# An encoder on one core: operand placement, the way into the MLP, PSUM banks, the head and the last down part rearranged

## The chip, the cores and the metric

The kernel runs on one core of a Trainium2 chip. The metric is device time in microseconds (us) of one launch. Engines are named as in the profile: PE is TensorE's matmul stream and PEld its weight loads, DVE is VectorE, ACT is ScalarE, POOL is GpSimd, SP is SyncE, whose queue issues most DMAs. A "q" behind a name (SPq) is that engine's own sequencer.

## The reference

Two encoder layers over 256 tokens of width 2048, with 256 memory tokens, all in float32. Cut to what matters:

```python
m = rms_norm(mem, mem_norm)
h = x
for i in range(2):
    n = rms_norm(h, attn_norm[i])
    # layer 0: 12 heads of 2-D neighbourhood attention with a bias; layer 1: grouped-query
    # attention with normalised, rotated q and k; both: 4 heads over the memory tokens (km, vm)
    z = n @ (a_w_in if i == 0 else b_w_in)
    km, vm = split(m @ w_mem_kv[i])
    h = h + concatenate([mix, cross]) @ w_o[i]
    n = rms_norm(h, mlp_norm[i])
    h = h + square(relu(n @ w_up[i])) @ w_down[i]      # 2048 -> 8192 -> 2048
return rms_norm(h, final_norm)
```

## The kernel before

**Numbers in two parts.** Every float32 matrix product is made of three products of rounded parts: each operand is split into a high part (`hi`, rounded on ACT by a copy, line 299) and a low part (`lo`, the rest, a subtraction on DVE, line 300), and hi·hi, hi·lo and lo·hi are summed in PSUM. Weights come from HBM in chunks of 128 x 2048 (1 MB, "raw") and are split in halves of 1024 columns. The normed inputs are split the same way and lie transposed, high and low side by side: `memT` (the memory), `nT` (input of a layer), `cat` (attention outputs), `hT` (input of the MLP). So each weight costs ACT and DVE one pass and PE three.

**Two kinds of product.** In "S" work (`s_products`, lines 211 to 222) the weights are stationary and the activations move: 512 wide against hi (line 218), 256 wide against lo (221). In "M" work (`m_products`, 198 to 209) the activations are stationary and the weights move, 512 wide: lines 205, 208, 209. The up projection (`u_products`, 664 to 672) has weights `uh`/`ul` stationary and `hT` moving, 256 wide: lines 670 to 672. In these names "moving operand" is the one that streams through PE, and the profile's matmul rows read `out<-moving,stationary`.

**The plan.** `run_all` (line 245) takes a list of pieces of work. Each has a load, a `pre` and a `prep` stage that are issued some pieces ahead (`ahead`, `SOON`), and a `run` stage with its matmuls. `later(n, ...)` puts small work n pieces ("ticks") behind. A scheduler orders what is written within the dependences; engines execute their own instructions in order.

**The stages.** The head (`begin`, 224) normalises `mem` and runs the first two chunks of the memory keys (`km`) side by side while their pieces of 256 KB arrive; then come the rest of the memory keys and values of both layers. Layer 0 makes qkv from `nT` and attends head by head; the output projection runs over `cat` (`add_o`, 644), 512 columns at a time; `o_done` (597) adds each result to h, and makes `hT` from the scaled h: copy by a scale on ACT (610), transposes on PE (317), split by gain on ACT and DVE (324, 325). The scale comes from the first three quarters of the columns, and `inv` (615) later corrects the output.

**The MLP.** Of 8 parts of d_ff, part 0's up products come first; then each step of parts 1 to 7's up products is interleaved with a down step of the part before (`add_mlp`, 887). A down step (`down_grains`, 740) is a 2 x 2 block product made in seven products (p1 to p7, Winograd's form): it loads four blocks of weights (b, t), makes sums of them (lines 758, 767, 768 on DVE, 759 by an accumulating DMA on POOL's queue), splits them into bh/bl and th/tl, and multiplies them with a_s, sums of the activation blocks, likewise split (`squared`, 716). The seven results stay in PSUM banks over half a part, and then go to h or to z (`taken`, 804; lines 802, 813, 815; `folded`, 820). The last part, part 7, is multiplied down in the plain way (`plain_grains`, 833): per 512 columns two chunks, the first split as two halves into the uh/ul buffers, the second as one piece of 2048 into th/tl, with a_p stationary. After that h is complete (`down_done`, 907), and in layer 1 `finish` (931) normalises and writes the last columns.

**Where things lie.** PSUM has 8 banks of 512 floats. `open_sums` (95) opens the pool `att` (4 banks, attention and transposes) and then `acc` (4 banks, sums). For parts 1 to 7 both are closed and one pool of 8 (`up` and p1 to p7) is opened (line 699). `wide` (418) holds nT0, hT0, nT1, hT1 one after the other; `half_of_side` (674) makes the uh/ul tiles, two buffers each.

Of the kernel before, what the change touches and what calls it, by code (L numbers as in the profile page):

```python
# [17 lines left out]
P = 128  # L18
# [16 lines left out]
HALF = CH // 2  # L35
GROUP = 2
PARTS = 8
PK = DFF // PARTS // P
STEPS = PK // 2
GUARD = 3  # L40
MASKED = -1e30

# [28 lines left out]
def encoder_kernel(ctx: ExitStack, tc: tile.TileContext, t: dict, out: bass.AP):  # L71
# [42 lines left out]
    mem0 = h.rearrange("p a b -> p (a b)")  # L114
    raws = [at.ring.tile([P, CH], F32, tag="raw", bufs=3, name=f"raw{c}") for c in range(2)]
    for j in range(8):
        s = slice(j * 512, (j + 1) * 512)
        nc.sync.dma_start(mem0[:, s], t["memT"][:, s])
        if j % 2 == 0:
            s = slice(j * 256, (j + 2) * 256)  # L120
            for c in range(2):
                nc.sync.dma_start(raws[c][:, s], t["w_km0"][c][:, s])
# [18 lines left out]
    def halves_of(w):  # L141

        tiles = {}

        def load():
            tiles["raw"] = loaded(w.src, "U")

        def prep_early(hf):
            tiles[hf] = half_of_side(tiles["raw"], hf)

        def prep(hf):
            if hf == 0:
# [24 lines left out]
        return [Grain(lambda: run(0), None, None, None, lambda: prep(0)),  # L177
                Grain(lambda: run(1), after, None, None, lambda: prep(1))]
# [45 lines left out]
    def begin():  # L224

        box["memT"] = at.cat.tile([P, KT, 512], F32R, tag="cat", name="memT")
        tiles = {}
        for w in plan[:2]:
            w.start(w)
        for q in range(4):  # L230
            for k in range(4 * q, 4 * q + 4):
                split_pair(box["memT"], mem0[:, k * SEQ : (k + 1) * SEQ], G_MEM, k)
                if k % 4 == 0:
                    for c, w in enumerate(plan[:2]):
# [4 lines left out]
            for c, w in enumerate(plan[:2]):  # L239
                s = slice(q % 2 * 512, q % 2 * 512 + 512)  # L240
                s_products(w, 4 * q, 4, *(x[:, s] for x in tiles[c]))
        for w in plan[:2]:
            w.done(w)

    def run_all():
        begin()
        for w in plan[2:]:
            order.extend([w] if isinstance(w, Grain) else halves_of(w))
# [25 lines left out]

    def add_m(srcs, acts, done):
        add_ms([(srcs, done)], acts, [(0, c) for c in range(len(srcs))])

# [3 lines left out]

    def add_ms(blocks, acts, order):

        ps = {}
        for n, (b, c) in enumerate(order):
            begins = all(o[0] != b for o in order[:n])

            def start(w, b=b, begins=begins):
                if begins:
                    ps[b] = [at.acc.tile([P, 512], F32, tag="acc", name="ps_m") for _ in range(NT)]  # L290
                w.ps = ps[b]
# [5 lines left out]
    def split(dst_hi, dst_lo, src):  # L297

        nc.scalar.activation(dst_hi, src, AF.Copy)  # L299
        nc.vector.tensor_tensor(dst_lo, src, dst_hi.bitcast(F32), op=ALU.subtract)  # L300

# [9 lines left out]
    def transposed(dst, src, ks, which):  # L311

        for a in range(0, len(ks), 2):
# [4 lines left out]
            for b, k in enumerate(ks[a : a + 2]):  # L318
                split_pair(dst, pt[:, b, :], which, k)

    def split_pair(dst, src, which, k):

        g = gain(which, k)
        nc.scalar.activation(dst[:, k, :SEQ], src, AF.Copy, scale=g)
        nc.vector.scalar_tensor_tensor(dst[:, k, SEQ:], src, g, dst[:, k, :SEQ].bitcast(F32),  # L325
                                       op0=ALU.mult, op1=ALU.subtract)
# [90 lines left out]

    def wide(name):
        return keep.tile([P, KT, 512], F32R, tag="wide", name=name)

# [60 lines left out]
    def add_mem(layer):  # L481
        for hd in range(NMH):
            add_s(t[f"w_km{layer}"][hd], get("memT"), km_done(layer, hd))
        add_m([t[f"w_vm{layer}"][c] for c in range(4)], parts_of("memT"), vm_done(layer))

# [98 lines left out]
    def sum_squares(which, i, nb):  # L584
        sq = at.side.tile([P, 512], BF16, tag="junk", bufs=2, name="sq")
        nc.scalar.activation(sq, h[:, i, nb * 512 : (nb + 1) * 512], AF.Square,
                             accum_out=ssq[which][:, i, nb : nb + 1])

    def mean_square(which, n, name):
# [5 lines left out]
        return v  # L595

    def o_done(layer, nb):
        which = 2 * layer

        def guard():  # L600
# [23 lines left out]
        def f(w):  # L624
            if nb == 0:
                closed("work")
                at.side = opened("side", side="right")
            for i in range(NT):
                hs = h[:, i, nb * 512 : (nb + 1) * 512]
                nc.vector.tensor_tensor(hs, w.ps[i], hs, op=ALU.add)  # L630
                if nb < 3:
                    sum_squares(which, i, nb)
            if nb == GUARD - 1:
                later(1, guard)
                for b in range(GUARD):
                    later(2 + 2 * b, scaled, b)
            if nb == 3:
# [46 lines left out]
    def up_grains(layer, part, m):  # L684
# [8 lines left out]
        def run(hf):  # L693
            if hf == 0:
                if part == 0:
                    own["ps"] = at.acc.tile([P, 512], F32, tag="acc", name="ps_u")[:, :SEQ]
                else:
                    if part == 1 and m == 0:
                        closed("ps_acc", "ps_att")
                        at.sums = opened("ps_sums", space=bass.MemoryType.PSUM)  # L700
# [39 lines left out]
    def down_grains(layer, part, n, begins, ends):  # L740
# [4 lines left out]
        def load():  # L745
# [4 lines left out]
            nc.sync.dma_start(own["t"][:, 0, :], src[:, 3 * 512 :])  # L750

        def block(k):

# [34 lines left out]
        def after_second():  # L788
# [44 lines left out]
    def plain_grains(layer, nb):  # L833
# [24 lines left out]
        def run(n):  # L858
# [5 lines left out]
            for i in range(NT):  # L864
                m_products(w, k0, nk, i, *own[c, hf], n == 0, n == 2)

        def after():
# [5 lines left out]
            for i in range(NT):  # L873
                for n, (c, hf, k0, nk) in enumerate(PIECES):
                    m_products(w, k0, nk, i, *own[c, hf], n == 0, n == 2, keep_order=True)
                w.done(w, i)

        return [Grain(lambda: run(0), None, lambda: load(0), None, lambda: prep(0, 0), SOON),
                Grain(lambda: run(1), None, None, None, lambda: prep(0, 1), SOON),
                Grain(lambda: run(2), after, lambda: load(1), None, lambda: prep(1, 0), SOON)]  # L880

# [25 lines left out]
    def down_done(layer, nb):  # L907
        def f(w):
# [161 lines left out]
    for j in range(8):  # L1070
        later(1 + j // 2, mem_squares, j)
    later(2, lambda: pin(nc.sync.dma_start(ident, t["ident"])))
    later(5, mem_stats)
    later(21, x_load)
# [124 lines left out]
```

## Time and profile before

| | |
|---|---|
| median of 3 runs | 2072.03 us (2071.43 to 2072.48) |
| the profiled execution | 2069.22 us, span 2067.2 us |
| granted TensorE clock in it | 0.997 |
| PE busy | 2039.7 us, 99% of the span |
| DVE busy | 1668.6 us, 81% |
| ACT busy | 1251.3 us, 61% |
| bytes moved | 433.78 MB, mean 210 GB/s |

How to read it: times are microseconds from the span's start. A row of the timeline gives start, duration, engine, line, operation, `out<-in`, and how many it groups; in brackets stands the idle time before it and what ended it. A duration of a matmul is longer than the time from its start to the next one's start, since they are pipelined; the pace is read from starts. A waits row gives the instruction that waited, what it waited for, the sum, the number and the longest of the waits. In the windows table a stretch is followed by its length, busy time and number of instructions of each engine, the granted clock of PE (1.00 is full), the share of DMA time, and GB/s.

### The profile page before, as it was taken

To read this page: it belongs to the slowest core of one execution; us is meant where nothing else is said; L and a number is where in the kernel's file an instruction comes from. 1 tells how busy PE (TensorE), PEld (TensorE's weight loads), DVE (VectorE), ACT (ScalarE), POOL (GpSimd) and SP (SyncE) were. 2 spreads that over 40 slices of the span, in tenths; PEclk is the share of its full clock that TensorE was granted. 3 is DMA by queue.
4 is the path that set the end of the run, shared out by engine and by line. 5 is a ranking of instruction groups with operands and counts; after the bars stand their busy time and mean duration, and the time that the engine had idled before them with its cause. 6 is when DMAs were issued, how large, how long until landed. Compare 5 with 4: busy or idle time off the path is not lost.

```text
span 2067.2 us, 31544 instructions
## 1 busy us (share of the span) xinstructions
PE 2039.7 (99%) x12516; PEld 1815.0 (88%) x12516; DVE 1668.6 (81%) x2047; ACT 1251.3 (61%) x1642; POOL 119.2 (6%) x144
## 2 busy tenths in 40 slices
PE   8999999999999999999999999999999999999998
PEld 6888888889999999999988888889999999999996
DVE  6767667566899999999996667666988999999896
ACT  6755555555666666666656557555666666666653
POOL 0000000000010000010000001000000000000000
PEclk9999999999999999999999999999999999999999
DMA  7755555736777787787765454536877787777773
GB/s 266 297 183 177 189 175 170 274 105 202 223 235 231 218 240 225 225 240 226 231 201 209 171 177 143 188 138 197 232 227 227 224 242 222 233 232 223 232 225 121
DMA packets 92996, 433.78 MB, mean 210 GB/s; under 512 B 10416, under 2 KB 12080, under 8 KB 59568
## 3 DMA queue, kind: packets, MB, share of 16 engines
q1 hardware_dynamic: 75456, 399.25, 57.3%
q0 software_dynamic: 16816, 31.46, 8.6%
q8 instruction: 98, 1.61, 0.3%
q10 hardware_dynamic: 576, 1.05, 0.1%
q14 instruction: 50, 0.41, 0.1%
HBM read 398.17 MB, written 4.19 MB: 195 GB/s over the span
## 4 chain that ended last, share of the span: by engine, by line
PE 97%; DVE 1%; issue 1%; DMA 1%; ACT 0%; SPq 0%; POOLq 0%; POOL 0%; DVEq 0%; ACTq 0%
PE ps_u L672 11%; PE ps_u L670 11%; PE ps_u L671 11%; PE p L779 9%; PE p L780 9%; PE p L781 9%; PE ps_m L205 8%; PE ps_m L208 8%; PE ps_m L209 8%; PE ps_s L218 7%; PE ps_s L221 3%; PE pt_a L379 1%; PE pt_n L317 0%; PE av L387 0%; PE sc_ps L353 0%
## 5 line engine op out<-in xcount | busy, mean ns | idle before, releaser
L671 PE MATMUL ps_u<-hT,uh 128*128 128x256 f32 x2048 | 569.3, 278 | 3.7 <-DVE hT L325 3.6
L670 PE MATMUL ps_u<-hT,uh 128*128 128x256 f32 x2048 | 569.9, 278 | 1.5 <-ACT uh L299 1.5
L672 PE MATMUL ps_u<-hT,ul 128*128 128x256 f32 x2048 | 569.3, 278 | 1.5 <-DVE ul L300 1.3
L299 ACT ACTIVATE uh<-raw_U 128x1024 fp32r<-128x1024 f32 x278 | 295.0, 1062 | 325.2 <-PE ps_u L671 301.9
L300 DVE TENSOR_TENSOR lo<-raw,hi 128x1024 fp32r<-128x1024 f32 (+1 forms) x222 | 266.3, 1204 | 167.7 <-ACT hi L299 166.4
L671 PEld LDWEIGHTS ps_u<-hT,uh 128*128 128x128 f32 x2048 | 385.9, 188 | 9.1 <-DVE hT L325 4.5
L670 PEld LDWEIGHTS ps_u<-hT,uh 128*128 128x128 f32 x2048 | 386.3, 189 | 7.6 <-ACT uh L299 1.9
L672 PEld LDWEIGHTS ps_u<-hT,ul 128*128 128x128 f32 x2048 | 387.1, 189 | 3.0 <-DVE ul L300 2.3
L300 DVE TENSOR_TENSOR ul<-raw_U,uh 128x1024 fp32r<-128x1024 f32 x278 | 337.9, 1219 | 35.4 <-ACT uh L299 35.4
L299 ACT ACTIVATE hi<-raw 128x1024 fp32r<-128x1024 f32 (+1 forms) x222 | 231.3, 1047 | 218.7 <-PE ps_m L209 116.1
L299 ACT ACTIVATE th<-t 128x2048 fp32r<-128x2048 f32 x112 | 215.2, 1921 | 124.9 <-PE p L781 118.2
L300 DVE TENSOR_TENSOR tl<-t,th 128x2048 fp32r<-128x2048 f32 x112 | 256.3, 2288 | 40.3 <-ACT th L299 39.9
L300 DVE TENSOR_TENSOR bl<-b,bh 128x1536 fp32r<-128x1536 f32 x112 | 196.1, 1751 | 0.4
L780 PE MATMUL p<-tl,a_s 128*128 128x512 f32 x448 | 177.2, 396 | 0.0
L781 PE MATMUL p<-th,a_s 128*128 128x512 f32 x448 | 174.4, 389 | 0.0
L299 ACT ACTIVATE bh<-b 128x1536 fp32r<-128x1536 f32 x112 | 166.2, 1484 | 6.4
L779 PE MATMUL p<-th,a_s 128*128 128x512 f32 x448 | 166.1, 395 | 0.0
L759 POOL DMA_DIRECT2D t<-b x112 | 97.0, 866 | 1168.3 <-DVE t L758 377.5
L218 PE MATMUL ps_s<-nT,hi 128*128 128x512 f32 x448 | 141.7, 394 | 0.0
L781 PE MATMUL p<-bh,a_s 128*128 128x512 f32 x336 | 131.1, 390 | 0.0
L780 PE MATMUL p<-bl,a_s 128*128 128x512 f32 x336 | 130.9, 390 | 0.0
L758 DVE TENSOR_TENSOR t<-t,b 128x512 f32<-128x512 f32 x112 | 77.2, 690 | 48.2 <-DMA t<-in_w_pair 36.4
(235 smaller groups left out, 3510.6 us busy)
## 6 DMA issues: line engine op xcount, KB each, us to landing
raw_U<-in_w_up SPq DMA_DIRECT2D x128, 1024.0 KB, 6.6
b<-in_w_pair SPq DMA_DIRECT2D x112, 768.0 KB, 4.5
raw<-in_w_o SPq DMA_DIRECT2D x32, 1024.0 KB, 5.0
t<-in_w_pair SPq DMA_DIRECT2D x112, 256.0 KB, 3.4
t<-b POOLq DMA_DIRECT2D x112, 256.0 KB, 6.6
raw<-in_w_b SPq DMA_DIRECT2D x21, 1024.0 KB, 5.0
raw<-in_w_av SPq DMA_DIRECT2D x12, 1024.0 KB, 4.9
raw<-in_w_aq SPq DMA_DIRECT2D x12, 1024.0 KB, 4.9
```

What stands on the lines that cost most here:

```text
L205: first = nc.tensor.matmul(w.ps[i], ah, hi[:, s], start=st, stop=False)
L208: nc.tensor.matmul(w.ps[i], ah, lo[:, s], start=False, stop=False)
L209: nc.tensor.matmul(w.ps[i], al, hi[:, s], start=False, stop=sp)
L218: nc.tensor.matmul(ps, hi[:, s], acts[:, k0 + j, :], start=k0 + j == 0, stop=False)
L299: nc.scalar.activation(dst_hi, src, AF.Copy)
L300: nc.vector.tensor_tensor(dst_lo, src, dst_hi.bitcast(F32), op=ALU.subtract)
L670: nc.tensor.matmul(ps, hi[:, s], acts[:, k, :SEQ], start=k == 0, stop=False)
L671: nc.tensor.matmul(ps, hi[:, s], acts[:, k, SEQ:], start=False, stop=False)
L672: nc.tensor.matmul(ps, lo[:, s], acts[:, k, :SEQ], start=False, stop=k == KT - 1)
L779: nc.tensor.matmul(ps, a[:, 0, ai, :], hi[:, s], start=begins, stop=False)
L780: nc.tensor.matmul(ps, a[:, 0, ai, :], lo[:, s], start=False, stop=False)
L781: nc.tensor.matmul(ps, a[:, 1, ai, :], hi[:, s], start=False, stop=ends)
```

## The change

1. **Moving operands elsewhere.** `wide` takes a byte offset: nT0 and nT1 begin 480 bytes into a tile that has grown by 512; hT0 and hT1 stay at its start. `half_of_side` takes one too: uh/ul tiles grow by 256 bytes, and where they are moving operands (the first w_b chunks and the plain part) they begin `MOVING_AT` = 160 bytes in. One of two "junk" buffers goes.
2. **Head.** `begin` runs three chunks side by side instead of two; the third buffer of "raw" is used from the start. The work behind it gets other ticks, and the sums of layer 0's memory values come from the att banks.
3. **PSUM.** `acc` is opened ahead of `att`, so it has banks 0 to 3 instead of 4 to 7.
4. **Way into the MLP.** The old h of the last 512 columns is scaled ahead (`begun`); when the last output product is there, one operation per tile adds it, scaled, to that straight from PSUM, and the transposes follow. The add to h itself, its squares and `inv` come 4, 6 and 8 ticks later and are issued behind the last hT split (`past`). The first two down steps' sums and splits are issued behind a split of up weights (`behind`).
5. **Plain part.** The second chunk is split in two halves too, into own tiles with the tags bh/bl and th/tl, and the work is four pieces instead of three.

```diff
-    def wide(name):
-        return keep.tile([P, KT, 512], F32R, tag="wide", name=name)
+    def wide(name, at=0):
+        room = keep.tile([P, KT * 512 + P], F32R, tag="wide", name=name)
+        return room[:, at // 4 : at // 4 + KT * 512].rearrange("p (a b) -> p a b", b=512)
...
-    def half_of_side(raw, hf):
-        tiles = tuple(at.side.tile([P, HALF], F32R, tag=n, bufs=2, name=n) for n in ("uh", "ul"))
-        split(*tiles, raw[:, hf * HALF : (hf + 1) * HALF])
+    def half_of_side(raw, hf, place=0):
+        s = slice(place // 4, place // 4 + HALF)
+        tiles = tuple(at.side.tile([P, HALF + 64], F32R, tag=n, bufs=2, name=n)[:, s] for n in ("uh", "ul"))
+        box.setdefault("splits", []).append(split(*tiles, raw[:, hf * HALF : (hf + 1) * HALF]))
         return tiles
...
-            tiles[hf] = half_of_side(tiles["raw"], hf)
+            tiles[hf] = half_of_side(tiles["raw"], hf, MOVING_AT)
...
-            box["nT"] = wide("nT0")
+            box["nT"] = wide("nT0", 480)
...
-                box["nT"] = wide("nT1")
+                box["nT"] = wide("nT1", 480)
...
     def open_sums():
+        at.acc = opened("ps_acc", space=bass.MemoryType.PSUM, bufs=4)
         at.att = opened("ps_att", space=bass.MemoryType.PSUM, bufs=4)
-        at.acc = opened("ps_acc", space=bass.MemoryType.PSUM, bufs=4)
...
+FIRST_CHUNKS = 3
...
-        for w in plan[:2]:
+        for w in plan[:FIRST_CHUNKS]:
...
-                later((5, 5, 1, 1)[hd], put, w)
+                later((12, 12, 13, 8)[hd], put, w)
...
+    def past(fn, ins=None):
+
+        a, v = ins or box["ready"]
+        with tc.issue_after(a.ins), tc.issue_after(v.ins):
+            fn()
...
+        def begun():
+
+            y = at.side.tile([P, NT, 512], F32, tag="T", bufs=2, name="h_s")
+            for i in range(NT):
+                nc.scalar.activation(y[:, i, :], h[:, i, D - 512 :], AF.Copy, scale=box["scale"][:, i : i + 1])
+            box["begun"] = y
...
             if nb == 3:
-                later(1, scaled, 3)
+                y = box["begun"]
                 for i in range(NT):
-                    sum_squares(which, i, nb)
-                later(2, inv)
+                    nc.vector.scalar_tensor_tensor(y[:, i, :], w.ps[i], box["scale"][:, i : i + 1], y[:, i, :],
+                                                   op0=ALU.mult, op1=ALU.add)
+                box["ready"] = transposed(box["hT"], lambda i, k: y[:, i, k % 4 * P : (k % 4 + 1) * P],
+                                          list(range(12, KT)), (G_M0, G_M1)[layer])
+                later(4, past, add)
+                later(6, past, squares)
+                later(8, past, inv)
...
+        def behind(fn):
+
+            return (lambda: past(fn, box["splits"][-4])) if part == 0 and n < 2 else fn
...
-        return [Grain(lambda: run("first", FIRST), lambda: after(FIRST), load, pre, prep_first, SOON),
-                Grain(lambda: run("second", SECOND), after_second, None, None, prep_second, SOON)]
+        return [Grain(lambda: run("first", FIRST), lambda: after(FIRST), load, behind(pre), behind(prep_first), SOON),
+                Grain(lambda: run("second", SECOND), after_second, None, None, behind(prep_second), SOON)]
...
-                own[c, hf] = half_of_side(own[0], hf)
+                own[c, hf] = half_of_side(own[0], hf, MOVING_AT)
             else:
-                own[c, hf] = tuple(at.mlp.tile([P, CH], F32R, tag=x, name=x) for x in ("th", "tl"))
-                split(*own[c, hf], own[1])
-
-        PIECES = ((0, 0, 0, 2), (0, 1, 2, 2), (1, 0, 4, 4))
+                own[c, hf] = tuple(at.mlp.tile([P, HALF], F32R, tag="bt"[hf] + x, name=f"{x}_p") for x in "hl")
+                split(*own[c, hf], own[1][:, hf * HALF : (hf + 1) * HALF])
+
+        PIECES = ((0, 0, 0, 2), (0, 1, 2, 2), (1, 0, 4, 2), (1, 1, 6, 2))
```

More of the change, by code (lines that the diff above doesn't have):

```diff
@@ L114, in encoder_kernel @@
     mem0 = h.rearrange("p a b -> p (a b)")
-    raws = [at.ring.tile([P, CH], F32, tag="raw", bufs=3, name=f"raw{c}") for c in range(2)]
+    raws = [at.ring.tile([P, CH], F32, tag="raw", bufs=3, name=f"raw{c}") for c in range(FIRST_CHUNKS)]
     for j in range(8):
@@ L120, in encoder_kernel @@
             s = slice(j * 256, (j + 2) * 256)
-            for c in range(2):
+            for c in range(FIRST_CHUNKS):
                 nc.sync.dma_start(raws[c][:, s], t["w_km0"][c][:, s])
@@ L233, in begin @@
                 if k % 4 == 0:
-                    for c, w in enumerate(plan[:2]):
+                    for c, w in enumerate(plan[:FIRST_CHUNKS]):
                         if q % 2 == 0:
@@ L246, in run_all @@
         begin()
-        for w in plan[2:]:
+        for w in plan[FIRST_CHUNKS:]:
             order.extend([w] if isinstance(w, Grain) else halves_of(w))
@@ L273, in add_s, with add_m, add_ms @@
         plan.append(Work("S", src, acts, 0, True, True, start, done))
-    def add_m(srcs, acts, done):
-        add_ms([(srcs, done)], acts, [(0, c) for c in range(len(srcs))])
+    def add_m(srcs, acts, done, banks=None):
+        add_ms([(srcs, done)], acts, [(0, c) for c in range(len(srcs))], banks)
     def parts_of(name):
         return lambda k, i: tuple(box[name][:, k, b * SEQ + i * P : b * SEQ + (i + 1) * P] for b in range(2))
-    def add_ms(blocks, acts, order):
+    def add_ms(blocks, acts, order, banks=None):
         ps = {}
@@ L289, in start @@
                 if begins:
-                    ps[b] = [at.acc.tile([P, 512], F32, tag="acc", name="ps_m") for _ in range(NT)]
+                    pool, tag = (at.att, "att") if banks else (at.acc, "acc")
+                    ps[b] = [pool.tile([P, 512], F32, tag=tag, name="ps_m") for _ in range(NT)]
                 w.ps = ps[b]
@@ L318, in transposed @@
             for b, k in enumerate(ks[a : a + 2]):
-                split_pair(dst, pt[:, b, :], which, k)
+                last = split_pair(dst, pt[:, b, :], which, k)
+        return last
     def split_pair(dst, src, which, k):
         g = gain(which, k)
-        nc.scalar.activation(dst[:, k, :SEQ], src, AF.Copy, scale=g)
-        nc.vector.scalar_tensor_tensor(dst[:, k, SEQ:], src, g, dst[:, k, :SEQ].bitcast(F32),
+        first = nc.scalar.activation(dst[:, k, :SEQ], src, AF.Copy, scale=g)
+        return first, nc.vector.scalar_tensor_tensor(dst[:, k, SEQ:], src, g, dst[:, k, :SEQ].bitcast(F32),
                                        op0=ALU.mult, op1=ALU.subtract)
@@ L483, in add_mem @@
             add_s(t[f"w_km{layer}"][hd], get("memT"), km_done(layer, hd))
-        add_m([t[f"w_vm{layer}"][c] for c in range(4)], parts_of("memT"), vm_done(layer))
+        add_m([t[f"w_vm{layer}"][c] for c in range(4)], parts_of("memT"), vm_done(layer), layer == 0)
     mem_sq = at.work.tile([P, 512], F32, tag="b_o", bufs=3, name="mem_sq")
@@ L627, in f, with add, squares @@
                 at.side = opened("side", side="right")
[L628 to L631, printed above, removed]
+            def add():
+                for i in range(NT):
+                    hs = h[:, i, nb * 512 : (nb + 1) * 512]
+                    nc.vector.tensor_tensor(hs, w.ps[i], hs, op=ALU.add)
+            def squares():
+                for i in range(NT):
                     sum_squares(which, i, nb)
+            if nb < 3:
+                add()
+                squares()
             if nb == GUARD - 1:
@@ L864, in run @@
             for i in range(NT):
-                m_products(w, k0, nk, i, *own[c, hf], n == 0, n == 2)
+                m_products(w, k0, nk, i, *own[c, hf], n == 0, n == 3)
         def after():
@@ L879, in plain_grains @@
                 Grain(lambda: run(1), None, None, None, lambda: prep(0, 1), SOON),
-                Grain(lambda: run(2), after, lambda: load(1), None, lambda: prep(1, 0), SOON)]
+                Grain(lambda: run(2), None, lambda: load(1), None, lambda: prep(1, 0), SOON),
+                Grain(lambda: run(3), after, None, None, lambda: prep(1, 1), SOON)]
     SOON = (8, 5, 4)
```

20 lines of the change are left out of this document (11 added, 9 removed).

## The prediction

> **What bounds the kernel now.** I read the page's chain first, then the windows by stage, then TensorE's waits.
>
> ```profile
> PE 97%; DVE 1%; issue 1%; DMA 1%; ACT 0%; SPq 0%; POOLq 0%; POOL 0%; DVEq 0%; ACTq 0%
> ...
> L671 PE MATMUL ps_u<-hT,uh 128*128 128x256 f32 x2048 | 569.3, 278 | 3.7 <-DVE hT L325 3.6
> ```
> ```profile
> 26.00:449.00 423.00, 423.00 (x2265) 363.31 (x2264) 282.67 (x422) 233.52 (x388) 3.15 (x4) 1.00 0.56 199
> 449.00:460.00 11.00, 7.94 (x53) 6.72 (x53) 9.07 (x16) 6.52 (x10) 0.88 (x1) 0.95 0.65 169
> 460.00:1073.00 613.00, 613.00 (x4168) 563.88 (x4168) 551.09 (x594) 390.39 (x401) 47.01 (x54) 1.00 0.76 226
> ...
> 1387.00:1398.50 11.50, 7.87 (x54) 6.67 (x54) 9.25 (x17) 6.54 (x10) 0.90 (x1) 0.96 0.68 161
> ```
> TensorE (PE) carries 97% of the chain. In the windows (length, then busy time of PE, PEld, DVE, ACT and POOL) it is busy without a gap over long stretches: 423.00 of 423.00, 613.00 of 613.00. It loses time in two ways only: at a few places it waits, and where it is busy its matmuls start one after the other at a pace that isn't everywhere the same. The waits:
>
> ```profile
> PE ps_s L218 <- ACT hi L299: 8.5, 2, 7.0
> PE ps_u L671 <- DVE hT L325: 3.6, 2, 2.1
> PE ps_u L670 <- ACT uh L299: 1.5, 2, 0.8
> PE ps_m L208 <- DVE tl L300: 1.3, 1, 1.3
> PE ps_u L672 <- DVE ul L300: 1.3, 2, 0.6
> ```
> Apart from the first 7.0 us, which no part of the change shortens, these waits (in us, with their number and the longest) come to 9.2 us. The pace is in this table, whose windows run from the start of one matmul to the start of the last of an unbroken run (length, PE busy, instructions touched; those that began before and still ran are taken off: two after 256-wide ones, else one):
>
> ```profile
> 57.26:79.43 22.17, 22.17 (x128) 1.00 0.89 368
> 202.87:213.36 10.49, 10.49 (x47) 1.00 0.49 148
> 338.55:347.84 9.29, 9.29 (x55) 1.00 0.40 121
> 387.26:428.96 41.70, 41.70 (x186) 1.00 0.70 274
> 714.28:719.58 5.30, 5.30 (x46) 1.00 0.94 283
> 1941.96:1947.31 5.35, 5.35 (x48) 1.00 0.95 279
> 2012.52:2017.89 5.37, 5.37 (x24) 1.00 0.91 340
> 2018.14:2023.38 5.24, 5.24 (x24) 1.00 0.59 205
> ```
> At the same granted clock (1.00), 512-wide matmuls cost 10.49/45 = 233.1 ns with nT stationary (203 us), 41.70/184 = 226.6 with cat stationary (387 us), 5.37/23 = 233.5 for uh/ul over a_p (2012 us) and 5.24/23 = 227.8 for th/tl over the same a_p (2018 us). Shapes and weight loads are equal; what differs is where the two operands lie. In the built program hi/lo, cat, memT, th/tl and a_p begin at byte 128 modulo 512 of a partition, nT at 160 and uh/ul at 480. So the pairs at 227 have equal remainders and those at 233 don't. The 256-wide products over hT have two paces too, 5.35/47 = 113.8 (1942 us) and 5.30/45 = 117.8 (714 us), with the same addresses: there the pace is not decided by addresses alone.
>
> **The change, part by part, against the profiled execution (2069.22 us; its span is 2067.2).** PE's chain is the sum, so I add what each part takes from or gives to PE.
>
> *A. nT moved by 480 bytes* (to remainder 128). M products over nT: 12 w_av and 21 w_b chunks of 24 matmuls, 792, each 233.1 − 226.6 = 6.5 ns: −5.1 us. Bounds: nothing (if the pace isn't set by this) and −5.1. S products, of both widths, start every 9.29/53 = 175.3 ns over nT (339 us) and 22.17/127 = 174.6 over memT (57 us): 28 chunks of 32, 896 × 0.7 ns, −0.6.
>
> *B. uh/ul as moving operands at +160 bytes.* 8 plain half-loads with 24 matmuls and three early w_b chunks, 264 × (233.5 − 227.8 = 5.7 ns) = −1.5. The tiles grow by 256 bytes, so the second buffer of each lies 256 off the first: only half may reach remainder 128. Bounds −1.5 and 0; I take −1.3, nearer the full row.
>
> *C. Way into the MLP.* Starts of the matmuls in layer 0:
>
> ```profile
> 453.58 0.28 PE L670 MATMUL ps_u<-hT,uh 128*128 128x256 f32 x1
> 454.61 0.39 PE L670 MATMUL ps_u<-hT,uh 128*128 128x256 f32 x1 [0.75 <-ACT uh L299]
> 454.83 0.28 PE L671 MATMUL ps_u<-hT,uh 128*128 128x256 f32 x1
> 456.64 0.38 PE L671 MATMUL ps_u<-hT,uh 128*128 128x256 f32 x1 [1.54 <-DVE hT L325]
> ...
> 457.86 0.28 PE L672 MATMUL ps_u<-hT,ul 128*128 128x256 f32 x1
> 458.77 0.55 PE L672 MATMUL ps_u<-hT,ul 128*128 128x256 f32 x1 [0.63 <-DVE ul L300]
> ```
> ```profile
> 453.23 0.69 DVE L758 TENSOR_TENSOR t<-t,b 128x512 f32<-128x512 f32 x1 [1.62 <-DMA t<-in_w_pair]
> 453.84 2.29 DVE L300 TENSOR_TENSOR tl<-t,th 128x2048 fp32r<-128x2048 f32 x1
> ```
> Against 0.12 per start, the three gaps lose 0.9, 1.7 and 0.8 us; with smaller ones around 450 us about 4.3. DVE, in order, sits behind a DMA of pair weights (1.62) and its 2.29 us split before it may make hT. The window of layer 1 at 1387 (11.50 us, 7.87 busy) is of the same kind, so about 9 us for two layers. The change puts the first two pair steps behind that hT split (`past`), scales the old h beforehand and adds straight from PSUM. What is late next: the split of up weights, 1.06 on ACT and then 1.22 on DVE, which waits for a buffer that PE frees. I leave 1.7 us per layer for it: −5.9 (bounds 0 and −9). The h add, squares and inv that are put off have DVE and ACT time in the stage after (551 of 613 us busy on DVE, 390 on ACT); if that cover goes, the 3 us or so of them (two adds like the 0.69 row, two squares, inv) delay the first down products.
>
> *D. Head, three chunks side by side.*
>
> ```profile
> 22.02 0.73 PE L218 MATMUL ps_s<-memT,hi 128*128 128x512 f32 x2 [1.42 <-ACT hi L299]
> 23.28 0.50 PE L221 MATMUL ps_s<-memT,lo 128*128 128x256 f32 x2 [0.53 <-DVE lo L300]
> ```
> After two chunks PE waits for the third's split, 1.42 and 0.53 us, and some 0.3 more in the matmuls that restart (0.50 us against 0.40 and less). With three, PE has half as much again to do in each quarter, and 5 loads of 256 KB instead of 4 to wait for, so the first 7.03 us stay and the same gap comes one chunk later: ACT still clears the sums of PSUM and splits chunk 3 (1.05, then 1.2 on DVE), while chunk 3's load, now behind raw0's last split on SP's queue, has come. About 1.4: −0.9 (bounds −2.3, and +1.5 if that load is late).
>
> *E. PSUM order.* The waits for h L802 and z L813, at the plain part of layer 0 only, come of ps_m lying in banks that p4 and p5 still hold. Their two starts come 0.62 and 1.11 us after the one before instead of 0.23 and lose 1.3:
>
> ```profile
> 1073.42 0.39 PE L781 MATMUL p<-th,a_s 128*128 128x512 f32 x1
> 1074.04 0.48 PE L205 MATMUL ps_m<-uh,a_p 128*128 128x512 f32 x1 [0.24 <-DVE z L813]
> ...
> 1075.29 0.40 PE L209 MATMUL ps_m<-uh,a_p 128*128 128x512 f32 x1
> 1076.40 0.50 PE L205 MATMUL ps_m<-uh,a_p 128*128 128x512 f32 x1 [0.72 <-DVE h L802]
> ```
> Other banks: −1.3. **It also adds a wait.** Between parts 0 and 1, p3 now takes the bank of the last up sums of part 0, two matmuls after them, and ACT splits uh before it empties that bank:
>
> ```profile
> 495.72 1.06 ACT L299 ACTIVATE uh<-raw_U 128x1024 fp32r<-128x1024 f32 x1 [1.62 <-PE ps_u L671]
> 496.68 0.36 ACT L723 ACTIVATE c<-ps_u 128x256 f32<-128x256 f32 x1
> ```
> From the freed buffer (495.7) to the end of the relu (497.0) are 1.3 us, less two matmuls: +1.2 in each layer, +2.4 (bounds 0 and +3). Behind p3's first stand 18 more p matmuls and then the rest of the up block; nothing on PE overtakes it.
>
> *F. Plain part in halves.* The last block waits 1.3 us for tl (list of waits), because th and tl are one 2048-wide split each. Halves in their own tags are free earlier and take half as long: −1.5, counting the start's delay (bounds 0 and −1.7).
>
> Sum: −5.1 − 0.6 − 1.3 − 5.9 − 0.9 − 1.3 + 2.4 − 1.5 = −14.2, so 2055.0 for a profiled execution. The median of the runs shown, 2072.03, lies 2.8 above the profiled one; so **2057.8**. My own range for this case is 2050 to 2066: A and B at nothing add 7, C at its ends +6 or −3.
>
> **The rivals.**
> 1. *The placement does nothing.* The pace could come of something else that differs between these stretches: in the 256-wide products it differs at equal addresses. Then A and B go and 2057.8 + 7.0 = 2064.8. Against it: th/tl and uh/ul over one a_p, back to back, in one layer. The Trainium skill, "TensorE: Matmul & The Clock Gate", section "Wait — 56ns, not 53.3ns?", gives the warm start-to-start time as the width over 2.4 GHz plus about 2.5 ns, 215.8 for 512, whatever the addresses; "SBUF — State Buffer", section "A bandwidth-pool intuition that's wrong (but worth ruling out)", gives the weight load a second, independent read port. By that rule this rival holds; the rows (226.6 and 233.1) agree with neither its figure nor its one pace.
> 2. *Half the up products slow down.* The 256 bytes of padding also move the second uh/ul buffer against hT in the 6144 up products (3 × 2048). If every block on it falls to the pace of the 714 us row: 3072 × 4.0 ns = +12.3, giving 2070.1, about no change. Against it: the blocks of before at 117.8 share their addresses with those at 113.8.
> 3. *All the up products slow down, and the kernel is slower.* Place: the up blocks of parts 1 to 7 as well. If the pace is decided by how a block enters, and the padding or the moved splits tip all of them: 6144 × 4.0 = +24.6, giving 2082.4. It decides from 14.2/24.6 = 58% of them on. For it: the pace of 117.8 occurs with no change of code. Against it: most blocks hold 113.8, and the order of the built program starts as many of them with ul as before (14 of 112 steps).
>
> **How the numbers follow.** A measurement of this kernel tells 0.2%, 4 us, from no change. Forecast 0.72, rival 1 0.13, rival 2 0.08, rival 3 0.07. The predicted time is the forecast's. The range 2049 to 2067 takes in the forecast's bounds and rival 1, and leaves rivals 2 and 3 and some ends of the forecast out. Faster: 0.70 of the forecast and 0.11 of rival 1, 0.81. Same: 0.02, 0.02 and 0.07 of rival 2, 0.11. Slower: 0.07 of rival 3 and 0.01 of rival 2, 0.08.
>
> **What would show it.** A: hi/lo over nT start every 226 to 228 ns. B: uh/ul over a_p too, perhaps on one buffer in two. C: no wait for hT by PE, one for uh or ul of about a microsecond. D: the wait for hi after three chunks, not two, and shorter. E: no wait for z or h at the plain part, a new one of p for the relu at each change from part 0 to 1. F: no wait for tl. The steady windows with 613.00 of 613.00 stay as long as before; if they grow by 6 or 12 us, rivals 2 or 3 hold and I am wrong.

## The result, and the profile after

| | before | changed |
|---|---|---|
| median of 4 runs | 2071.73 us (2070.39 to 2072.48) | 2054.27 us (2053.93 to 2054.78) |
| ratio | | 0.9917, 95% interval 0.9899 to 0.9934 |
| span of the profiled execution | 2067.2 us | 2052.1 us |

The changed kernel is 17.5 us faster by the medians and 15.1 by the two spans; 2057.8 was forecast, with 14.2 us off the profiled execution. The forecast held, and in the right order of size for most of its terms. Three things behind it did not: equal remainders are no general rule for the pace, one term was put to the wrong part alone, and a loss of clock behind the way into the MLP went unseen. Each experiment below came with executions of its own of the kernel before, whose medians are 2069.83 to 2071.17 us, so kernels of different experiments are compared by ratios or by stages. One execution of experiment 2's kernel took 2253.24 us at a granted clock of 0.848 and is left out of its numbers.

PE still carries the chain. Its waits in the changed kernel (what waited, for what, us in total, times, longest):

```profile
PE ps_s L221 <- ACT hi L303: 7.7, 2, 6.8
PE p L816 <- ACT c L756: 2.1, 2, 1.1
PE ps_u L704 <- DVE ul L304: 1.8, 3, 0.8
PE av L392 <- ACT pT L303: 1.0, 1, 1.0
PE ps_s L224 <- DVE lo L304: 0.5, 1, 0.5
```

The waits for hT, uh, tl, h and z are gone; ul is waited for in three places, 1.8 us in all; and p waits for c, the relu (line 756 now), once in each layer: the wait that was added. Lines have moved by 3 to 38, so 670 to 672 are 702 to 704 here, and 299 and 300 are 303 and 304.

The paces in the changed kernel, windows read as before (length, PE busy, instructions touched, granted clock, DMA share, GB/s):

```profile
201.12:211.33 10.21, 10.21 (x47) 1.00 0.52 144
452.92:485.57 32.65, 32.64 (x287) 1.00 0.61 202
1140.37:1149.43 9.06, 9.06 (x41) 1.00 0.33 108
...
1959.99:1965.35 5.36, 5.36 (x48) 1.00 0.83 232
1999.64:2042.93 43.29, 43.29 (x192) 1.00 0.35 128
```

Over nT: 10.21/45 = 226.9 ns in layer 0 and 9.06/40 = 226.5 in layer 1, where the stretch of before had 233.1. The whole plain part of layer 1, uh/ul pieces and the others, is one run of 192 matmuls without a break, 43.29/191 = 226.6 ns, over both uh/ul buffers. The steady up products stay at 5.36/47 = 114.0.

The way into the MLP, which lost 0.9, 1.7 and 0.8 us at 453 to 459 us, in the changed kernel:

```profile
451.67 0.39 PE L702 MATMUL ps_u<-hT,uh 128*128 128x256 f32 x1
451.89 0.28 PE L703 MATMUL ps_u<-hT,uh 128*128 128x256 f32 x1
452.93 0.38 PE L704 MATMUL ps_u<-hT,ul 128*128 128x256 f32 x1 [0.76 <-DVE ul L304]
```

This is the one large gap that is left there: 1.04 us from start to start, 0.9 lost to the up weights' split. With the small ones of 0.2 to 0.4 us before and after it, the starts between 442 and 454 us are 1.76 us late in all; counted in the same way, those of before were 5.29 late between 444.5 and 459.5 us. And there the loss of before did not end. These are its windows right behind the last large gap of each layer, and then those behind the way in of the changed kernel:

```profile
459.50:462.20 2.70, 2.70 (x15) 0.50 0.93 291
1398.50:1401.00 2.50, 2.50 (x14) 0.52 0.91 282
```
```profile
454.00:470.00 16.00, 16.00 (x144) 1.00 0.58 197
1386.00:1400.00 14.00, 14.00 (x121) 1.00 0.55 201
```

In the kernel before the granted clock was 0.50 and 0.52 there, and the up products started about 0.21 us apart (459.55, 459.76, 459.97) instead of 0.113: about 1.2 us more in each layer. In the changed kernel it stayed at 1.00. Counted against 113.4 ns for each of the first 100 up products, the starts are 6.6 and 7.0 us late in the two layers of before, and 1.9 and 2.0 in the changed kernel.

The head, where the wait now stands behind three chunks:

```profile
24.86 0.40 PE L224 MATMUL ps_s<-memT,lo 128*128 128x256 f32 x2
26.13 0.73 PE L221 MATMUL ps_s<-memT,hi 128*128 128x512 f32 x2 [0.87 <-ACT hi L303]
```

And the wait that was added, in layer 0:

```profile
488.85 0.28 PE L702 MATMUL ps_u<-hT,uh 128*128 128x256 f32 x1
488.97 0.28 PE L703 MATMUL ps_u<-hT,uh 128*128 128x256 f32 x1
490.31 0.50 PE L816 MATMUL p<-bh,a_s 128*128 128x512 f32 x1 [1.06 <-ACT c L756]
```
```profile
488.93 1.06 ACT L303 ACTIVATE uh<-raw_U 128x1024 fp32r<-128x1024 f32 x1 [0.23 <-PE ps_u L703]
489.90 0.37 ACT L756 ACTIVATE c<-ps_u 128x256 f32<-128x256 f32 x1
```

From 488.97 to 490.31 are 1.34 us instead of 0.12: 1.2 lost, because ACT does 1.06 us of uh first.

**Where the time came from.** The next table cuts PE's time at the same instructions in each trace (the first S product over nT0, the first M over cat, the first up product of a layer, the first plain product of a layer, the last matmul's end). Over the kernels of all experiments, the attention, projection and last plain stages repeat within 0.1 us where nothing in them differs, so the table tells parts apart there that medians of runs cannot. Two stages repeat less well: the memory products take 92.95 to 94.23 us with the same three chunks, and an up-and-pair stage of the same code 626.00 to 626.93, for a reason that is left open below; 0.8 us of layer 1's 626.92 is of this kind.

| stage, us | before | changed | difference | parts in it |
|---|---|---|---|---|
| to the first matmul | 7.03 | 6.78 | −0.25 | |
| memory products | 94.28 | 93.06 | −1.22 | head |
| layer 0, attention | 249.07 | 247.85 | −1.23 | nT0 |
| output projection of layer 0 | 94.42 | 94.40 | −0.02 | |
| layer 0, up and pair steps | 629.24 | 626.09 | −3.15 | way in, PSUM |
| layer 0, plain part, and layer 1, attention | 199.62 | 194.95 | −4.67 | nT1, uh/ul, PSUM |
| output projection of layer 1 | 109.62 | 109.59 | −0.03 | |
| layer 1, up and pair steps | 629.24 | 626.92 | −2.31 | way in, PSUM |
| layer 1, plain part | 46.18 | 43.68 | −2.50 | uh/ul, halves |

### The profile page after: what moved, and what is told of

Read it like the earlier page. It is cut to its first block, busy times and chain, and to the rows that moved or that the text cites. A ratio compares the mean times of both kernels' runs of the same rounds, so it can differ in the third digit from the quotient of the medians.

```text
span 2052.1 us, 31583 instructions
## 1 busy us (share of the span) xinstructions
PE 2029.9 (99%) x12516; PEld 1812.2 (88%) x12516; DVE 1669.2 (81%) x2061; ACT 1252.7 (61%) x1652; POOL 119.3 (6%) x144
## 4 chain that ended last, share of the span: by engine, by line
PE 97%; ACT 1%; DVE 1%; issue 0%; DMA 0%; SPq 0%; POOLq 0%; POOL 0%; ACTq 0%
PE ps_u L704 11%; PE ps_u L702 11%; PE ps_u L703 11%; PE p L816 9%; PE p L817 9%; PE p L818 9%; PE ps_m L208 8%; PE ps_m L211 8%; PE ps_m L212 8%; PE ps_s L221 6%; PE ps_s L224 3%; PE pt_a L384 1%; PE pt_n L321 1%; DMA raw<-in_w_km 0%; PE av L392 0%
## 5 line engine op out<-in xcount | busy, mean ns | idle before, releaser
L303 ACT ACTIVATE hi<-raw 128x1024 fp32r<-128x1024 f32 (+1 forms) x224 | 231.7, 1039 | 210.4 <-PE ps_m L212 117.8
```

Of the source, the lines that this page charges most:

```text
L303: first = nc.scalar.activation(dst_hi, src, AF.Copy)
```

## The experiments

My theory was the prediction's: each part acts on its own stage, the pace is set by equal remainders, and the stalls at the way in come of the order on DVE and ACT. The rivals stand in each expectation.

**1. nT back (e1_nT_back).** The changed kernel with
```diff
-            box["nT"] = wide("nT0", 480)
+            box["nT"] = wide("nT0")
```
and the same for nT1.

> The changed kernel with nT0 and nT1 back at the start of their tiles (remainder 160 against 128 of hi and lo); all else as changed. Theory (the pace is set by where the two operands lie): M matmuls over nT go from about 227 to 233 ns, 792 of them, so 4.2 us of pace come back and the time is 2058.5 +- 0.7. Rival (the pace comes of something else in these stretches, the shift was idle): 2054.3, and the matmuls over nT stay at 227.

Measured: 2058.96 us, ratio to before 0.9946 (0.9932 to 0.9961). Its windows of the same two stretches:

```profile
201.37:211.86 10.49, 10.49 (x47) 1.00 0.48 147
1142.16:1151.49 9.33, 9.33 (x41) 1.00 0.31 109
```

10.49/45 = 233.1 and 9.33/40 = 233.3 ns, as before. The stage of layer 0's attention is 249.08 instead of 247.85, that with layer 1's attention 198.06 instead of 194.95: 1.2 + 3.1 = 4.3 us for the two offsets. The placement does it; the rival (the shift was idle) falls.

**2. Placement alone (e2_place_only).** The kernel before with `wide(name, at)`, 480 for nT0 and nT1, the padded uh/ul tiles with 160 where they move, and one junk buffer.

> The kernel before with the placement alone: nT0 and nT1 480 bytes in, uh and ul tiles 256 bytes larger and 160 bytes in where they move, one junk buffer. Theory: 4.2 us over nT and 1.6 us over a_p and for the first w_b chunks, so 5.8 us faster than before, 2066. Rival (the buffer 256 bytes off keeps 233): 5.0 us. Rival (no effect of placement): as before, 2071.7. The waits for hT, z, h and tl stay as in the kernel before in every case.

Measured: 2063.98 us, the median of six, ratio 0.9972 (0.9960 to 0.9984), 5.8 us by the ratio. Layer 0's attention is 247.86, as in the changed kernel, and of the waits of before all are there, though those for ul come to 0.3 us instead of 1.3. Three of them:

```profile
PE ps_u L674 <- DVE hT L327: 3.8, 2, 2.0
PE ps_u L673 <- ACT uh L301: 1.5, 2, 0.8
PE ps_m L210 <- DVE tl L302: 1.4, 1, 1.4
```

So placement and waits are separate gains: placement gives the pace, and the waits for hT, uh, tl, h and z stay. Its up-and-pair stages were 1.9 and 1.0 us longer than before in the profile, which is of the slowest of the six: in layer 0 part 0's block ran at 117.8 ns instead of 113.4, and the granted clock behind the way in was low for longer (0.73 over 459 to 464 us, 0.50 over 1395 to 1400). The steady up products kept 114 ns, so the padding did not slow them. Both uh/ul buffers run at 227 over a_p, though one lies 256 bytes off; the rival with half the gain falls.

**3. Way in as before (e3_entry_back).** The changed kernel with `later(1, scaled, 3)`, squares and `later(2, inv)` as before, no `begun`, and
```diff
-            return (lambda: past(fn, box["splits"][-4])) if part == 0 and n < 2 else fn
+            return fn
```

> The changed kernel with the way into the MLP as before: the last 512 columns are added to h, then scaled, then transposed; inv and squares at once; the first two down steps are not held behind the splits. Theory (the in-order DVE and ACT queues with pair work ahead of the hT split made the stalls): the waits for hT, uh and ul return, about 4 us in each layer, time 2062 +- 1. Rival (banks or placement took the stalls away, not the order): below 2056.

Measured: 2059.54 us, ratio 0.9951 (0.9936 to 0.9966). The waits:

```profile
PE ps_u L690 <- DVE hT L330: 3.4, 2, 1.9
PE ps_u L689 <- ACT uh L303: 1.5, 2, 0.8
```

hT and uh are back, and so is the low clock, here in layer 1:

```profile
1390.00:1395.00 5.00, 5.00 (x32) 0.67 0.91 262
```

In the ten experiments that keep the new way in, and in the changed kernel, the granted clock is 1.00 over the same stretch of both layers. The experiment undoes the way in as a whole; which of its pieces does how much was not separated. The two up-and-pair stages are 628.21 and 629.14, 2.1 and 2.2 us above the changed kernel (3.0 in layer 1 against experiment 1, whose block of part 0 ran at the same 113.4 ns), not the 4 each that I expected. What I had not seen: p's wait for the relu is not in this kernel's list at all, so the undoing also took away 2.5 us of loss. In its trace 24 up products stand between the last up sums of part 0 and p3, as in the kernel before; in the changed kernel two do.

**4. PSUM as before (e4_psum_back).** The changed kernel with att opened ahead of acc.

> The changed kernel with the pools of PSUM opened as before (att first, then acc). Theory: the wait of p for the relu between parts 0 and 1, 2.1 us in two, goes, the wait at the plain part of layer 0 for z and h, about 1.3 us, comes back: net 0.8 us faster than the changed kernel, 2053.5. Rival (the scheduler fills the gap with the same work and another wait follows): 2054.3 to 2055.6.

Measured: 2052.83 us, ratio 0.9917 (0.9903 to 0.9932): the same as the changed kernel. Its waits trade places as expected:

```profile
PE ps_m L208 <- DVE h L839: 0.8, 1, 0.8
...
PE ps_m L208 <- DVE z L850: 0.2, 1, 0.2
```

No wait of p for c; the plain part of layer 0 waits for h and z again, and its stage is 196.09 instead of 194.95, 1.1 us. The PSUM part of the change thus gave 1.1 and took 2.5, the two starts of p that are gone (1.2 us each). The median does not show these 1.4 us; in the profile, part 0's block of layer 0 ran at 117.8 ns, which takes some of them.

**5. p4 in that bank (e7_p4_bank).** The changed kernel, in which p4's tile is allotted right behind the first `up` tile, so p3 gets the next bank:
```diff
+                    if part == 1 and m == 0:
+                        box["early"] = at.sums.tile([P, 512], F32, tag="p4", name="p4")
```

> The changed kernel, in which p4 instead of p3 takes the bank of the last up sums of part 0. Theory (p3 waits for the relu that empties this bank, and p4 comes 4 us later): the wait of p for c goes, 2.1 us in two, and nothing takes its place: 2052.2. Rival (another bank or operand is late by as much): 2054.3.

Measured: 2050.64 us, ratio 0.9903 (0.9888 to 0.9918). The wait for c is gone from the list and only a 0.2 us one has come:

```profile
PE ps_u L704 <- DVE ul L304: 2.1, 4, 0.8
PE av L392 <- ACT pT L303: 1.0, 1, 1.0
PE ps_s L224 <- DVE lo L304: 0.5, 1, 0.5
PE p L820 <- DVE tl L304: 0.2, 1, 0.2
```

The up-and-pair stages are 624.69 and 625.52, 1.4 us below the changed kernel in each. In layer 0 that is the wait. In layer 1 it is not the wait alone: part 0's block ran at 113.4 ns here and at 117.8 in the changed kernel, and against experiment 1, where it ran at 113.4 too (626.10), 0.6 us are left, because some 0.6 are lost at and behind the new wait for tl (1882 to 1886 us). Whether p4's bank brings that wait about was not tried. Of the kernels tried this has the lowest median and the lowest ratio; its interval and that of the changed kernel overlap, the stages do not. Against experiment 3 it is 3.5 and 3.6 us shorter: that is the way in without the wait that came with it.

**6. Head as before (e5_head_back).** `FIRST_CHUNKS = 2`, the ticks of before, the memory value sums in acc.

> The changed kernel with the head as before: two chunks side by side, the ticks of before, the sums of layer 0's memory values in the acc banks. Theory (with three chunks the same gap comes later and is shorter): PE's waits for hi and lo of the third chunk come back at about 20 us, 1 to 1.5 us lost, 2055.5 +- 0.4. Rival (the third load delays the start by as much as the gap shortens): 2054.3.

Measured: 2053.71 us, ratio 0.9920 (0.9905 to 0.9935): not above the changed kernel, and my 2055.5 is missed. The memory stage is 94.42, and the wait for the split after two chunks is back: the two waits for hi come to 7.8 us with 6.4 for the first, so 1.4 for the second, against 0.9 in the changed kernel. The 1.4 us between the two stages are more than that is worth: the stage is 92.95 to 94.23 in the eleven profiles with three chunks and 94.28 to 94.74 in the three with two. But the sums of layer 0's memory values no longer shift the rotation of acc. In the built program the last up sums of layer 0 lie in bank 3 and p3 in bank 1, where the changed kernel has both in bank 1, and p waits in layer 1 alone:

```profile
PE p L816 <- ACT c L756: 1.1, 1, 1.1
```

The up-and-pair stage of layer 0 is 624.76 instead of 626.09, 1.3 less, and pays for the head. Also, the head's gain is not steady: the first product over nT0 starts at 99.8 to 100.8 us in the six profiles of experiments 1, 3, 4, 5 and 7 and of the changed kernel, and at 100.8 to 101.3 in the three with two chunks: about 0.9 us, with the first matmul itself anywhere from 6.3 to 7.0.

**7. Plain part as before (e6_plain_back).** One split of 2048 columns, three pieces.

> The changed kernel with the second chunk of each plain piece split as one piece of 2048 into th and tl, as before. Theory (halves in tags of their own are free earlier and take half as long): the wait for tl in the last block comes back, 1.5 to 1.8 us, 2055.9. Rival (the wait went because the work behind it moved): 2054.3, no wait for tl.

Measured: 2056.15 us, ratio 0.9931 (0.9915 to 0.9948), and the wait is back:

```profile
PE ps_m L211 <- DVE tl L304: 1.4, 1, 1.4
```

The plain stage of layer 1 is 45.71 instead of 43.68: 2.0 us, against the 1.5 of the prediction.

**8 and 9. Other offsets of nT (s1_nT_256_128, s2_nT_64).** The changed kernel with `wide("nT0", 224)` and `wide("nT1", 96)`; then with 32 and 416.

> The changed kernel with nT0 224 and nT1 96 bytes into their tiles, so that hi and lo, as moving operands, lie 256 bytes (layer 0) and 384 bytes (layer 1, 128 modulo 256) off nT modulo 512. Theory (equal remainders modulo 256 give the short pace): 227 ns in layer 0 and 230 to 234 in layer 1. Rival, modulo 512: 230 to 234 in both. Rival, modulo 128: 227 in both.

> The changed kernel with nT0 32 and nT1 416 bytes in, so that hi and lo lie 448 bytes (192 modulo 256) off nT in layer 0 and 64 off in layer 1. Theory (modulo 256): 230 to 234 ns in both layers, the time 2056 to 2058.5. Rival, modulo 64: 227 in both and 2054.3. A graded law would show a different pace for either sign.

Measured, one execution each: 2057.76 and 2054.82 us. The windows of the first, then of the second:

```profile
201.14:211.35 10.21, 10.21 (x47) 1.00 0.49 147
1195.02:1226.75 31.73, 31.73 (x137) 1.00 0.50 174
```
```profile
200.85:211.34 10.49, 10.49 (x47) 1.00 0.48 149
1193.06:1224.20 31.14, 31.14 (x137) 1.00 0.48 172
```

By the difference of moving and stationary start, modulo 256 bytes: 256 gives 226.9 ns like 0, so the period is 256 or a part of it; 128 gives 31.73/136 = 233.3; 192 gives 233.1; 64 gives 31.14/136 = 229.0. It is a graded law, and modulo 128 falls.

**10 to 12. Offsets of hT (s3_hT_64, s4_hT_128_192, e8_p4_hT_32_224).** The up products have the weights stationary and hT moving, 256 wide. The changed kernel with `wide(f"hT{layer}", 64)`; with 128 and 192 for the two layers; and experiment 5's kernel with 32 and 224.

> The changed kernel with hT0 and hT1 64 bytes into their tiles, so that hT and uh or ul have equal remainders modulo 256 in the up products (192 modulo 256 in the changed kernel). Theory (equal remainders hold the short pace however a block begins): the blocks that begin with ul go from 117.7 to about 113.5 ns and the steady ones from 114.0 to 113.5, 3 us from 740 matmuls of 4 ns and 2.5 us from 5000 of 0.5: 2048.5 to 2051.5. Rival (the 256 wide pace is decided by how a block begins): 2054.3. Rival (with equal addresses a block can only lose): 2056 or more.

> The changed kernel with hT0 128 and hT1 192 bytes into their tiles: hT lies 64 (layer 0) and 128 (layer 1) off uh and ul modulo 256, where the changed kernel has 192 and 0 gave 119.9 ns. Theory (a graded law of the difference): a pace between 113.5 and 119.9 in both layers, not the same in both. Rival (only equal remainders are bad, all others have the two paces 113.8 and 117.7): 114.0 in the steady steps of both layers, 117.7 where a block begins with ul, 2054.3.

> The kernel with p4 in the bank of the last up sums (2050.64 us), and hT0 32 and hT1 224 bytes into their tiles: hT lies 224 (layer 0) and 160 (layer 1) off uh and ul modulo 256, on both sides of the 192 of the changed kernel. So far the steady pace of the up products is 119.9 ns at 0, 117.8 at 64, 118.6 at 128, 114.0 at 192. Theory (192 lies in a range of good differences): 113.3 to 115 ns on one side at least, 2049 to 2052, faster than the kernel with p4 alone if blocks that begin with ul fall below 117 too. Rival (192 alone is good): 117 to 119 on both sides, 10 us or more in each layer, 2070.

Measured: 2082.34 us, ratio 1.0053 (1.0037 to 1.0070); 2071.11 in one execution; 2068.21, ratio 0.9987 (0.9977 to 0.9997). Steady blocks of 48 up products, one in each layer, in this order of kernels:

```profile
600.05:605.68 5.63, 5.63 (x48) 1.00 0.54 196
1502.97:1508.60 5.63, 5.63 (x48) 1.00 0.50 192
```
```profile
608.23:613.77 5.54, 5.54 (x48) 1.00 0.64 227
1505.14:1510.71 5.57, 5.57 (x48) 1.00 0.79 258
```
```profile
607.65:613.20 5.55, 5.55 (x48) 1.00 0.63 229
1504.72:1510.24 5.52, 5.52 (x48) 1.00 0.85 256
```

| difference modulo 256 | 0 | 64 | 128 | 160 | 192 | 224 |
|---|---|---|---|---|---|---|
| up products, ns (length/47) | 119.8 | 117.9 | 118.5 | 117.4 | 114.0 | 118.1 |

Here equal remainders are the worst of six, and 192, which both kernels have, is the best. My theory that equal is good fell with the first of these runs, by 28 us; the one that 192 lies in a range fell with the last.

## Why the prediction was right, and where it was not

*What bounds the kernel.* Right: the time came out of waits of PE and out of its pace. The windows that were without a gap before got shorter only where nT or uh/ul were read, and behind the way in, where the clock had been low.

*A, nT.* Right in its cause (experiments 1 and 2), too large in size: −5.1 and −0.6 were forecast, 4.3 us were measured by undoing it, the first w_b chunks included. The term was one pace, taken from an unbroken run, times all 792 matmuls. The starts of the hi and lo products over nT, summed over the trace, go from 185.9 to 181.8 us, 5.3 ns for each and not 6.5: the rest of them stand in short runs between attention work. S products gained nothing (157.2 us of starts before, 157.3 after); the 0.7 ns between two stretches was no effect of the address.

*B, uh/ul.* −1.3 forecast; the a_p runs go from 233.5 to 226.6 ns on both buffers. For 192 matmuls that is 1.3 us, and the starts of the first w_b chunks sum to 0.2 less. Half a gain was feared for the buffer 256 off, and s1 shows why it did not come: 256 acts like 0.

*C, the way in.* Right in mechanism, too small: 5.9 forecast; 7.1 by experiments 3 and 5 together (3.5 + 3.6). What would be left was well told: 1.7 us in each layer forecast, 1.76 and 1.75 measured, most of it the wait for ul that was named. In layer 1 the 3.6 would be some 0.6 larger without the wait for tl in experiment 5. The mis-sized term is what was there before: the working has about 4.3 in layer 0 and about 9 in both, and it was 5.3 in layer 0 up to 459.5 us and 6.6 with the stretch at a granted clock of 0.50 behind it (7.0 in layer 1). That stretch had no term: the row 460 to 1073 us gives 1.00, because a mean over 613 us hides 2 us. The prediction's own figures also give 5.6 (9 less 2 times 1.7), not the 5.9 that stands in the sum.

*D, the head.* −0.9 forecast, 1.2 in the stage of these two traces, about 0.9 over nine profiles. Single profiles of one head differ by as much, so no more than the sign and the rough size is shown.

*E, PSUM.* The gain of 1.3 was 1.1 (experiment 4). The loss of 2.4 was 2 times 1.2, the best sized term of all. But the step "PSUM order. It also adds a wait" put the whole loss to the order of the pools, though its text names the two matmuls as well, and it takes two causes: p3 in the bank of the last up sums, and p3 only two matmuls behind them. Experiment 3 has the bank without the place (24 matmuls between) and no wait; experiment 4 has the place without the bank and no wait; experiment 6 has both in one layer and waits in that one.

*F, plain halves.* −1.5 forecast, 2.0 measured.

*What was luck.* 2.8 us of the forecast are the distance of the median of three from the profiled execution before. The changed kernel has no such distance (2054.27 against 2053.93), and the medians of before in the later comparisons are lower, so 15.6 to 16.9 us would be the gain by those. Without the 2.8 the forecast is 2055.0, within 0.7 of the median. The parts came to the right sum because their errors have both signs: A with its S products was put 1.4 us too high, C and F together 1.7 or more too low.

*The rivals.* That placement does nothing is refuted by experiment 1. The Trainium skill, "TensorE: Matmul & The Clock Gate", section "Wait — 56ns, not 53.3ns?", has one warm start-to-start time for a width; this case has 226.6, 229.0 and 233.3 for 512 and 114.0 to 119.8 for 256 at a granted clock of 1.00, with nothing moved but an operand's address. Rivals 2 and 3 did not come: the padding of uh/ul is 256 bytes, and the difference to hT stays at 192 modulo 256. But a slowdown of all the up products, which they priced at 24.6 us, does exist: experiment 10 brought it about by the address, with 28 us. Had hT been aligned together with nT, by the same reasoning by which I approved of nT, the change would have been slower than the kernel before.

*The part left open.* At 192 the up products have two paces, 114.0 and 117.7. One block, part 0's up products of layer 1, fell to the second in the changed kernel's profile:

```profile
455.00:485.00 30.00, 30.00 (x267) 1.00 0.63 212
1390.00:1420.00 30.00, 30.00 (x256) 1.00 0.62 197
```

267 instructions in 30 us of layer 0, 256 in 30 us of layer 1. In experiment 1 neither layer's block does it, in experiment 2 that of layer 0; in the eleven profiles with this difference it is 7 blocks of 22. It costs about 0.8 us of the stage (626.92 against 626.10 in experiment 1) and I have no cause for it that a run shows. For the shorter blocks of the steps the record has a pattern: in the same eleven profiles all 1056 blocks of 48 that begin with a product over uh ran at 113.5 to 114.0 ns, and of the 124 of 46 that begin with one over ul, 107 ran at 117.7 to 117.8 and 17 at 113.8 to 114.1. So the pace goes with how a block begins, but not in every case, and no run moved the beginning by itself.

## What to carry to other kernels

Where an engine is busy without a gap, read its pace from starts, not from durations, and compare stretches of equal shape: 3% were in the addresses of two operands. Try an offset on each kind of product by itself, since the one that helps M products (0) was the worst for the up products. And when a change moves both where a result lies and when the next one asks for it, look at what the two do together: neither alone cost anything here, together 2.5 us. And after a gap, read the granted clock in a window of a few us: over 613 us it read 1.00, though the first 2 us of them were at 0.50.

## What the runs showed of the hardware

In M work and in the up products the pace of fp32r matmuls at full granted clock depends on the difference of the two operands' start addresses, with a period of 256 bytes as far as 0 against 256 shows. S products did not change when their difference went from 32 to 0 (157.2 and 157.3 us in all). 512 wide with the weights moving: 226.9 ns at 0, 229.0 at 64, 233.3 at 128, 233.1 at 192 and at 224 (nT of before). 256 wide with the weights stationary: 119.8 at 0, 117.4 to 118.5 at 64, 128, 160 and 224, and 114.0 or 117.7 at 192. Which of the two paces a block takes at 192 isn't told by this difference. At 128 too one long block differed, with 120.0 against 118.5 in the steady ones. What in the chip makes the difference was not tried.

After three waits of PE of 0.6 to 2.1 us within some 6 us, the granted clock was 0.50 and 0.52 over windows of 2.7 and 2.5 us (kernel before, both layers), and the products started 0.21 us apart; where only one wait of 0.8 us was left, it stayed at 1.00 (changed kernel). How much waiting it takes was not tried.
